# A two-branch layer in fp32: the first block's norm from feature-major tiles alone, and one more step in its scans

## The chip, the cores and the metric

The kernel runs on one core of one Trainium2 chip. The metric is the device time of one execution, in microseconds (us), as the median of three timed executions: 2352.43 us for the kernel before (2352.43, 2354.13 and 2346.6). One more execution was recorded by the hardware profiler, and all views of the trace are of that one.

## The reference

The input is 2048 tokens of 1024 features with 16 learned meta tokens ahead of them. One hybrid layer follows: an RMS norm, one combined projection, a Mamba-2 (SSD) branch and a gated linear attention (GLA) branch beside each other, and a gated merge. What this case touches is the norm at the start and the meta tokens' part of the SSD branch:

```python
def rmsnorm(x, w):
    xf = x.astype(jnp.float32)
    y = xf * lax.rsqrt(jnp.mean(xf * xf, axis=-1, keepdims=True) + EPS)
    return (y * w).astype(x.dtype)

def hybrid_layer(hres, ...):
    u = rmsnorm(hres, norm_w)
    proj = jnp.einsum('bld,dn->bln', u, w_in)
    z, xbc, dt_raw, q, k, v, g_gla, a_lr, merge_g = split_cols(proj, IN_WIDTHS)
...
    s0 = jnp.zeros((b, SSD_HEADS, SSD_HEAD_DIM, SSD_STATE), jnp.float32)
    y_m, s_m = ssd_chunked(xs[:, :m], dt[:, :m], a, bm[:, :m], cm[:, :m], N_META, s0)
    y_r, _ = ssd_chunked(xs[:, m:], dt[:, m:], a, bm[:, m:], cm[:, m:], SSD_CHUNK, s_m)
...
    return hres + jnp.einsum('bld,de->ble', merged, w_out)
```

`m` is 16, so the SSD state after the meta tokens (`s_m`) is the state with which the real tokens begin. Everything is fp32.

## The kernel before

**Stages.** Stage 1 (to about 1550 us of the trace) makes all projections and both branches, in four blocks of 512 tokens; block 0 also has the 16 meta tokens, 528 columns in all. Stage 2 makes the merge gates, the branch projections and the output projection.

**Matmuls.** An fp32 operand is split into a high and a low half of type f32r (ACT copies the high half, another engine subtracts to get the low one), and `accum` (L184 to L188) adds three products: high with high, high with low, low with high. So each projection of a tile is 8 k-tiles times 3 products times the number of its column pieces. In block 0, `load_w` (L164 to L177) also loads each weight raw into a `wr` buffer (SP's DMA queue), splits it on ACT (L173) and POOL (L174) into one of four `whl` buffers, and a later `load_w` stores the pair back to memory (k_...), from which the other blocks load it.

**The start.** `load_u` (L238 to L295) makes u, the normed input, feature-major in 8 column tiles (k-tiles). For block 0 SP first issues the row loads: four of 128 tokens and one of the meta tokens, from `xm`. ACT squares each with an accumulated sum (L250), DVE scales the sum (L259), POOL raises it to −0.5 (L260), and four PE matmuls with the identity (L273), and one for the meta tokens (L277), spread the five factor columns over all partitions in PSUM. Then for each of the 8 column tiles (128 features by 528 tokens, from the transposed copy `xmt`): DMA on SP, two multiplications on DVE (L289, 16 and 512 columns, with the factors in PSUM), the high half on ACT (L291), a store of the normed tile for the next stage on ACT's DMA queue (L292), the low half on DVE (L293). Small constants come behind it: `hv` (L308), three copies of `gw2` into one buffer of the pool "act" (L324), a mask of 448 KB (L331).

**Generators.** In stage 1 the branches' scans are Python generators. The loop over groups and heads runs the projection generators `ssd_proj` and `gla_proj`, and at each of their yields `step()` advances every running scan by one yield. So a yield in a scan decides beside which projection its instructions are put. PE and SP (the queue of weight loads) run in exactly this written order; ACT, DVE and POOL are ordered by the scheduler of the tile framework. The SSD projection of a group is z (token-major, `proj_tok`, with a yield at its half) and four feature tiles (`proj_feat`, one yield each), whose convolution is on DVE (three instructions of L471, then L475).

**The scan.** `ssd_scan` handles the four chunks of 128 tokens of one group. For block 0 it first transposes the meta tokens' rows (L500); one step later come the four score products of the chunks (L516) and `before(0)` (three transposes, L532, and DVE and ACT work on them); then `meta_state` (L506 to L511) multiplies the meta tokens into PSUM (L509) and DVE copies the state to `s_ssd` (L511), directly ahead of `before(1)` and `after(0)`. `after(c)` has the matmuls L556 (within the chunk), L557 (with `s_ssd`) and L559 (the chunk's addition to the state). Behind the last `after` are the row factors (POOL, L230), ACT's scaling (L585) and, a step later, PE's transposes of the finished rows (L590).

**Buffers.** PSUM has three banks for projections (pj), three for transposes (pt) and two for scans (pc). Pools named here: "act" has 8 buffers and "tok4" 5.

## Time and profile before

| what | us |
|---|---|
| runs | 2352.43, 2354.13, 2346.6 (median 2352.43) |
| profiled execution | 2356.86 |
| its span | 2355.0 (1.86 around it) |
| PE busy / DVE busy / ACT busy / POOL busy | 2255.4 / 1562.0 / 1189.1 / 684.2 |
| first matmul of the first projection | 15.74 |
| first matmul of the second projection | 47.49 |

A row of the timeline gives the start and the duration in us, the engine, the line, the operation, the tile written and the tiles read, shapes, and in square brackets the idle time of the engine before it and what ended that. "x8" counts instructions; an fp32 matmul appears as two. A row of the windows gives a stretch and its length, then the busy time of PE, of PE's weight loads, of DVE, ACT and POOL in it, the granted clock of PE as a share of full speed, the busy share of the DMA engines, and GB/s. Groups give busy time, mean ns of one, then idle time before them and its releaser. A row of DMA issues ends with KB and the us from issue to landing.

### The profile page before, as it was taken

To read this page: it belongs to the slowest core of one execution; us is meant where nothing else is said; L and a number is where in the kernel's file an instruction comes from. 1 tells how busy PE (TensorE), PEld (TensorE's weight loads), DVE (VectorE), ACT (ScalarE), POOL (GpSimd) and SP (SyncE) were. 2 spreads that over 40 slices of the span, in tenths; PEclk is the share of its full clock that TensorE was granted. 3 is DMA by queue.
4 is the path that set the end of the run, shared out by engine and by line. 5 is a ranking of instruction groups with operands and counts; after the bars stand their busy time and mean duration, and the time that the engine had idled before them with its cause. 6 is when DMAs were issued, how large, how long until landed. Compare 5 with 4: busy or idle time off the path is not lost.

```text
span 2355.0 us, 36504 instructions
## 1 busy us (share of the span) xinstructions
PE 2255.4 (96%) x12641; PEld 1968.2 (84%) x12641; DVE 1562.0 (66%) x2889; ACT 1189.1 (50%) x2764; POOL 684.2 (29%) x681
## 2 busy tenths in 40 slices
PE   6899999999999999999999999889999999999998
PEld 6889889888888988888988898768788788777886
DVE  4676665676675667566558555664679854788876
ACT  4665655465544455543455443454554454544543
POOL 3343433122321212221122200207424254322441
PEclk8999999999999999999999999989999999999999
DMA  8665875666786666787666655456668866778752
GB/s 274 212 215 183 296 255 192 202 220 218 248 282 191 207 224 208 254 268 221 193 217 216 206 167 163 136 181 226 218 222 275 277 215 213 253 244 274 236 192 108
DMA packets 301546, 518.06 MB, mean 220 GB/s; under 512 B 27696, under 2 KB 143664, under 8 KB 301360
## 3 DMA queue, kind: packets, MB, share of 16 engines
q1 hardware_dynamic: 200112, 402.32, 52.7%
q10 hardware_dynamic: 101248, 113.41, 13.8%
q8 instruction: 99, 1.62, 0.3%
q14 instruction: 87, 0.71, 0.1%
HBM read 368.42 MB, written 147.19 MB: 219 GB/s over the span
## 4 chain that ended last, share of the span: by engine, by line
PE 66%; DMA 12%; DVE 10%; ACT 5%; issue 4%; POOL 2%; SPq 1%; ACTq 0%; DVEq 0%; POOLq 0%
PE pj L186 11%; PE pj L188 11%; PE pj L187 11%; PE psa L186 4%; PE psa L187 4%; PE psa L188 4%; PE psb L187 2%; PE psb L188 2%; PE psb L186 2%; DMA acc<-in_xmt 2%; PE pc L556 2%; DMA br<-br_t 2%; PE pc L690 1%; DVE b L894 1%; PE pc L780 1%
## 5 line engine op out<-in xcount | busy, mean ns | idle before, releaser
L186 PE MATMUL pj<-u,whl 128*128 128x512 f32 (+1 forms) x1184 | 447.4, 378 | 8.3 <-ACT g_all L429 3.3
L188 PE MATMUL pj<-u,whl 128*128 128x512 f32 (+1 forms) x1184 | 431.6, 365 | 0.8 <-POOL whl L174 0.8
L187 PE MATMUL pj<-u,whl 128*128 128x512 f32 (+1 forms) x1184 | 430.7, 364 | 0.0
L186 PE MATMUL pj<-whl,u 128*128 128x256 f32 (+1 forms) x992 | 291.5, 294 | 8.1 <-ACT u L291 5.5
L188 PE MATMUL pj<-whl,u 128*128 128x256 f32 (+1 forms) x992 | 285.2, 287 | 0.7 <-DVE u L293 0.7
L187 PE MATMUL pj<-whl,u 128*128 128x256 f32 (+1 forms) x992 | 285.1, 287 | 0.6 <-POOL whl L174 0.5
L186 PE MATMUL psa<-b,a 128*128 128x512 f32 x640 | 253.5, 396 | 19.0 <-ACT sn L934 17.0
L186 PEld LDWEIGHTS pj<-u,whl 128*128 128x128 f32 x1184 | 225.7, 191 | 46.2 <-ACT g_all L429 3.7
L188 PEld LDWEIGHTS pj<-u,whl 128*128 128x128 f32 x1184 | 225.2, 190 | 36.8 <-POOL whl L174 1.1
L187 PEld LDWEIGHTS pj<-u,whl 128*128 128x128 f32 x1184 | 225.7, 191 | 33.3
L187 PE MATMUL psa<-b,a 128*128 128x512 f32 x640 | 252.8, 395 | 0.0
L188 PE MATMUL psa<-b,a 128*128 128x512 f32 x640 | 252.5, 395 | 0.0
L918 DVE TENSOR_TENSOR a<-ar,a 128x512 fp32r<-128x512 f32 x160 | 151.1, 950 | 82.1 <-ACT a L917 81.9
L186 PEld LDWEIGHTS pj<-whl,u 128*128 128x128 f32 x992 | 192.3, 194 | 9.2 <-ACT u L291 6.0
L187 PEld LDWEIGHTS pj<-whl,u 128*128 128x128 f32 x992 | 192.4, 194 | 1.7 <-POOL whl L174 1.3
L188 PEld LDWEIGHTS pj<-whl,u 128*128 128x128 f32 x992 | 192.4, 194 | 1.5 <-DVE u L293 1.5
L80 POOL TENSOR_TENSOR wr<-wr 128x256 f32<-128x256 f32 x80 | 67.0, 838 | 432.0 <-DMA wr<-y 172.1
L174 POOL TENSOR_TENSOR whl<-wr,whl 128x512 fp32r<-128x512 f32 (+1 forms) x100 | 133.5, 1342 | 188.9 <-ACT whl L173 141.3
L908 POOL TENSOR_TENSOR as<-ar,ar 128x512 f32<-128x512 f32 x40 | 59.3, 1482 | 422.4 <-DMA ar<-in_w_feat 124.3
L894 DVE TENSOR_TENSOR b<-br,b 128x512 fp32r<-128x512 f32 x196 | 149.2, 784 | 45.3 <-ACT b L893 44.8
L471 DVE SCALAR_TENSOR_TENSOR acc<-cin,hcw,acc 128x512 f32<-128x512 f32 (+1 forms) x192 | 156.6, 816 | 24.7 <-ACT acc L467 24.1
L893 ACT ACTIVATE b<-br 128x512 fp32r<-128x512 f32 x196 | 119.1, 626 | 93.5 <-DMA br<-br_t 34.7
(267 smaller groups left out, 5077.9 us busy)
## 6 DMA issues: line engine op xcount, KB each, us to landing
whl<-k_s SPq DMA_DIRECT2D x96, 512.0 KB, 4.4
whl<-k_g SPq DMA_DIRECT2D x96, 512.0 KB, 4.1
whl<-k_v SPq DMA_DIRECT2D x48, 512.0 KB, 3.8
whl<-k_z SPq DMA_DIRECT2D x36, 512.0 KB, 3.8
wr<-in_w_feat SPq DMA_DIRECT2D x64, 256.0 KB, 4.5
k_s<-whl SPq DMA_DIRECT2D x32, 512.0 KB, 3.6
cb<-cumd ACTq DMA_DIRECT2D x64, 256.0 KB, 5.6
y<-gg ACTq DMA_DIRECT2D x64, 256.0 KB, 4.5
```

The source lines that it names most:

```text
L80: nc.gpsimd.tensor_tensor(o, x, y, op=ALU.subtract)
L174: nc.gpsimd.tensor_tensor(hl[:, 1], raw, hl[:, 0].bitcast(F32), op=ALU.subtract)
L186: nc.tensor.matmul(ps, sh, mh, start=first, stop=False, **kw)
L187: nc.tensor.matmul(ps, sh, ml, start=False, stop=False, **kw)
L188: nc.tensor.matmul(ps, sl, mh, start=False, stop=last, **kw)
L471: nc.vector.scalar_tensor_tensor(acc, cin[:, k:k + tt], hcw[:, ti, k:k + 1], acc, op0=ALU.mult, op1=ALU.add)
L556: nc.tensor.matmul(py[:, h * 64:(h + 1) * 64], dm[:, h], xdt[:, h], start=True, stop=True)
L690: nc.tensor.matmul(ps[:, r * P:(r + 1) * P], kq[:, 2 * r * P:(2 * r + 1) * P], kq[:, (2 * r + 1) * P:(2 * r + 2) * P], start=True, stop=True)
L893: nc.scalar.activation(t[:, 0], raw, AF.Copy)
L894: nc.vector.tensor_tensor(t[:, 1], raw, t[:, 0].bitcast(F32), op=ALU.subtract)
L908: nc.gpsimd.tensor_tensor(s1, a21, a22, op=ALU.add)
L918: nc.vector.tensor_tensor(t[:, 1], src, t[:, 0].bitcast(F32), op=ALU.subtract)
```

## The change

1. **First block from columns alone.** `first_u` takes the place of `load_u` for block 0. The row loads from `xm` are gone. The eight column tiles are asked for at once, into eight buffers of the pool "act", the even ones by SP and the odd ones by ACT's queue. ACT squares each tile (L268), seven DVE additions sum them over the k-tiles (L270), five PE matmuls with a column of ones sum over partitions (L275), and one DVE (L277) and one POOL instruction (L279) make all five factor columns. The broadcast to all partitions is the same as before (L282, L284), but ACT copies it into one SBUF tile of 528 columns, so that `to_u` multiplies each tile with one DVE instruction (L248).
2. **Stores of u.** Block 0's stores of the normed tiles go to SP's queue, one behind each raw weight load from the third on, instead of ACT's queue.
3. **A buffer.** The staging of `gw2` comes from the pool "acc" and no longer from "act".
4. **The meta state a step apart.** A `yield` behind `meta_state()` in `ssd_scan`, in block 0 alone: everything of a scan behind the meta state comes one step of `step()` later.

```diff
@@ load_w
             nc.sync.dma_start(raw, src)
+            if u_stores and len(kept) > 2:
+                nc.sync.dma_start(*u_stores.pop(0))
             nc.scalar.activation(hl[:, 0], raw, AF.Copy)
@@ new functions
+    def to_u(b, kt, xk, rbc, uh, ul):
+        m0 = 0 if b else META
+        nc.vector.scalar_tensor_tensor(xk, xk, norm_w[:, kt:kt + 1], rbc, op0=ALU.mult, op1=ALU.mult)
+        nc.scalar.activation(uh[:, kt, :m0 + BLK], xk, AF.Copy)
+        if b:
+            nc.scalar.dma_start(u_left[b][kt], xk[:, m0:])
+        else:
+            u_stores.append((u_left[b][kt], xk[:, m0:]))
+        nc.vector.tensor_tensor(ul[:, kt, :m0 + BLK], xk, uh[:, kt, :m0 + BLK].bitcast(F32), op=ALU.subtract)
+
+    def first_u():
+        tt = META + BLK
+        uh, ul = u_pair(tt)
+        xs = []
+        for kt in range(KT):
+            xs.append(mk(wk, [P, META + BLK], F32, "act", bufs=NACT))
+            (nc.scalar if kt % 2 else nc.sync).dma_start(xs[kt], xmt[:, kt, :tt])
+        nc.sync.dma_start(cst[:, :2], cf32[:, :2])
+        nc.sync.dma_start(pv, pvec)
+        sq = [mk(wk, [P, 2, META + BLK], F32, "tok4", bufs=NT4) for _ in range(KT // 2)]
+        total = sq[0][:, 0]
+        for kt in range(KT):
+            nc.scalar.activation(sq[kt // 2][:, kt % 2], xs[kt], AF.Square)
+            if kt:
+                nc.vector.tensor_tensor(total, total, sq[kt // 2][:, kt % 2], op=ALU.add)
+        at = [META + c * P for c in range(NCH)] + [0]
+        n = len(at)
+        ps = bank(pt, "pt")
+        for i, a in enumerate(at):
+            nc.tensor.matmul(ps[:, 2 * i:2 * i + 2], total[:, a:a + P], ones[:, :2], start=True, stop=True)
+        r = mk(sm, [P, n], F32, "rs5", bufs=1)
+        nc.vector.tensor_scalar(r, ps[:, :2 * n].rearrange("p (i two) -> p i two", two=2)[:, :, 0], 1.0 / D, EPS,
+                                op0=ALU.mult, op1=ALU.add)
+        nc.gpsimd.tensor_tensor(r, r, mhalf[:, 0:1].to_broadcast([P, n]), op=ALU.pow)
+        rb, rm = bank(pt, "pt"), bank(pt, "pt")
+        for c in range(NCH):
+            nc.tensor.matmul(rb[:, c * P:(c + 1) * P], r[:, c:c + 1].to_broadcast([P, P]), ident,
+                             start=True, stop=True)
+        nc.tensor.matmul(rm[:, :META], r[:META, NCH:].to_broadcast([META, P]), ident[:META, :META],
+                         start=True, stop=True)
+        rbc = mk(wk, [P, 3 + META + BLK], F32, "cin")[:, :tt]
+        nc.scalar.activation(rbc[:, :META], rm[:, :META], AF.Copy)
+        nc.scalar.activation(rbc[:, META:], rb, AF.Copy)
+        for kt in range(KT):
+            to_u(0, kt, xs[kt], rbc, uh, ul)
+        return uh, ul
@@ load_u: the part for block 0 taken out
-            if m0:
-                xt = mk(wk, [P, D], F32, "tok4", bufs=NT4)
-                nc.sync.dma_start(xt[:n], xm[r0:r0 + n, :])
-                nc.scalar.activation(xt[:n], xt[:n], AF.Square, accum_out=ss[:n])
...
-    for _ in fetch_u(0):
-        pass
+    next_u[0] = first_u()
@@
-    w2r = mk(wk, [P, META + BLK], F32, "act", bufs=NACT)[:48, :512]
+    w2r = mk(wk, [P, META + BLK], F32, "acc")[:48, :512]
@@ ssd_scan
         if m0:
             meta_state()
+            yield
```

**The order on DVE at the start.** Rows of the order are: line, operation, output and inputs with buffer numbers, shape; x4 counts equal ones. Lines are those of each kernel's own file. Before, from the first multiplication of a column tile on (`acc_298`, `acc_305`, `acc_312` are column tiles, `u_253` holds u, `w_372` the gate weights of gw2):

```order
L289 SCALAR_TENSOR_TENSOR acc_298<-acc_298,pv,pt_291 128x512
L289 SCALAR_TENSOR_TENSOR acc_305<-acc_305,pv,pt_291 128x512
L320 TENSOR_SCALAR nega<-nega 128x16
L289 SCALAR_TENSOR_TENSOR acc_298<-acc_298,pv,pt_296 128x16
L289 SCALAR_TENSOR_TENSOR acc_305<-acc_305,pv,pt_296 128x16
L327 TENSOR_TENSOR w_372<-act_368,w_372 16x512
L332 CAST msk<-tok_29_376 128x896
L293 TENSOR_TENSOR u_253<-acc_298,u_253 128x528
L293 TENSOR_TENSOR u_253<-acc_305,u_253 128x528
L289 SCALAR_TENSOR_TENSOR acc_312<-acc_312,pv,pt_296 128x16
L289 SCALAR_TENSOR_TENSOR acc_312<-acc_312,pv,pt_291 128x512
```

In the change, from the last addition of squares on (`tok_11_272` the sum, `act_254` to `act_268` the eight column tiles, `cin_307` the factor tile):

```order
L270 TENSOR_TENSOR tok_11_272<-tok_11_272,tok_14_275 128x528
L360 CAST msk<-tok_21_356 128x896
L277 TENSOR_SCALAR rs_16_297<-pt_291 128x5
L248 SCALAR_TENSOR_TENSOR act_254<-act_254,pv,cin_307 128x528
L248 SCALAR_TENSOR_TENSOR act_256<-act_256,pv,cin_307 128x528
L248 SCALAR_TENSOR_TENSOR act_258<-act_258,pv,cin_307 128x528
L248 SCALAR_TENSOR_TENSOR act_260<-act_260,pv,cin_307 128x528
L248 SCALAR_TENSOR_TENSOR act_262<-act_262,pv,cin_307 128x528
L248 SCALAR_TENSOR_TENSOR act_264<-act_264,pv,cin_307 128x528
L248 SCALAR_TENSOR_TENSOR act_266<-act_266,pv,cin_307 128x528
L248 SCALAR_TENSOR_TENSOR act_268<-act_268,pv,cin_307 128x528
L254 TENSOR_TENSOR u_253<-act_254,u_253 128x528
```

Each tile's low half (L293) came behind the tile's multiplications before; now all eight multiplications stand ahead of the first low half (L254), and the last addition behind the gate weights (L355, the row ahead of these).

**The order on PE at the meta state of group 0.** Before, behind the last matmul of a feature tile's projection (`pj_1133`, `pj_1134` its banks):

```order
L188 MATMUL pj_1134<-u_253,whl_1166 128x264
L509 MATMUL pc_1211<-c_120_1081,bt_1083 128x256
L532 MATMUL pt_1216<-cst,act_673 128x128
L532 MATMUL pt_1216<-cst,act_763 128x128
L532 MATMUL pt_1216<-cst,act_849 128x128
L556 MATMUL pc_1234<-c_128_1100,sq_1107 128x64 x4
L557 MATMUL pc_1234<-s_ssd,act_927 128x256
L559 MATMUL pc_1240<-c_129_1102,bt_1105 128x256
L186 MATMUL pj_1257<-u_253,whl_1259 128x264
```

In the change, the same place (L537 is the line that was L509; `pj_1208` and `pj_1209` are the banks of the next projection):

```order
L190 MATMUL pj_1122<-u_253,whl_1154 128x264
L537 MATMUL pc_1199<-c_112_1069,bt_1071 128x256
L188 MATMUL pj_1208<-u_253,whl_1210 128x264
L189 MATMUL pj_1208<-u_253,whl_1210 128x264
L190 MATMUL pj_1208<-u_253,whl_1210 128x264
L188 MATMUL pj_1209<-u_253,whl_1210 128x264
L189 MATMUL pj_1209<-u_253,whl_1210 128x264
L190 MATMUL pj_1209<-u_253,whl_1210 128x264
L188 MATMUL pj_1208<-u_253,whl_1210 128x264
```

The transposes, chunk products and state matmuls that followed the meta state directly now stand behind the 48 matmuls of the next projection.

**The order on PE at the end of group 0's scan.** Before, behind the last matmul of group 1's z (`pj_1613`); `tok_124_1092` holds the finished rows:

```order
L188 MATMUL pj_1613<-whl_1698,u_253 128x256
L590 MATMUL pt_1757<-cst,tok_124_1092 128x128 x4
L590 MATMUL pt_1765<-cst,tok_124_1092 128x128 x4
L500 MATMUL pt_1773<-cst,act_1208 16x128
L500 MATMUL pt_1773<-cst,act_1332 16x128
L500 MATMUL pt_1773<-cst,act_1453 16x128
L516 MATMUL pc_1781<-act_1585,act_1453 128x128 x4
L532 MATMUL pt_1792<-cst,act_1208 128x128
L532 MATMUL pt_1792<-cst,act_1332 128x128
L532 MATMUL pt_1792<-cst,act_1453 128x128
L186 MATMUL pj_1810<-u_253,whl_1812 128x264
```

In the change, the same place, and then the end of the next projection:

```order
L190 MATMUL pj_1584<-whl_1679,u_253 128x256
L528 MATMUL pt_1745<-cst,act_1196 16x128
L528 MATMUL pt_1745<-cst,act_1283 16x128
L528 MATMUL pt_1745<-cst,act_1404 16x128
L544 MATMUL pc_1753<-act_1538,act_1404 128x128 x4
L560 MATMUL pt_1764<-cst,act_1196 128x128
L560 MATMUL pt_1764<-cst,act_1283 128x128
L560 MATMUL pt_1764<-cst,act_1404 128x128
L188 MATMUL pj_1782<-u_253,whl_1784 128x264
```

```order
L190 MATMUL pj_1783<-u_253,whl_1815 128x264
L619 MATMUL pt_1860<-cst,tok_116_1080 128x128 x4
L619 MATMUL pt_1868<-cst,tok_116_1080 128x128 x4
L537 MATMUL pc_1876<-c_218_1749,bt_1751 128x256
L188 MATMUL pj_1879<-u_253,whl_1881 128x264
```

The eight transposes of finished rows (L590, now L619) have moved from ahead of group 1's scan steps to behind the next projection (banks `pj_1782` and `pj_1783`), where they stand ahead of group 1's meta state.

More of the change, by code (lines that the diff above doesn't have):

```diff
@@ L235, in split, with u_pair @@
         nc.vector.tensor_tensor(lo, src, h.bitcast(F32), op=ALU.subtract)
-    def load_u(b):
-        m0 = META if b == 0 else 0
-        row0 = META - m0 + b * BLK
-        tt = m0 + BLK
-        pair = mk(upool, [P, 2, KT * (META + BLK)], F32R, "u")[:, :, :KT * tt]
-        uh, ul = [pair[:, i].rearrange("p (k t) -> p k t", k=KT) for i in range(2)]
+    u_stores = []
+    def u_pair(tt):
+        pair = mk(upool, [P, 2, KT * (META + BLK)], F32R, "u")[:, :, :KT * tt]
+        return [pair[:, i].rearrange("p (k t) -> p k t", k=KT) for i in range(2)]
@@ L264, in load_u @@
         for c in range(NCH):
[L265 removed]
+            rs.append(rows_rstd(row0 + c * P, P))
             yield
[L267 to L270 removed]
         rb = bank(pt, "pt")
@@ L273, in load_u @@
             nc.tensor.matmul(rb[:, c * P:(c + 1) * P], rs[c].to_broadcast([P, P]), ident, start=True, stop=True)
[L274 to L293 removed]
+        rbc = mk(wk, [P, 3 + META + BLK], F32, "cin")[:, :BLK]
+        nc.scalar.activation(rbc, rb, AF.Copy)
+        yield
+        for kt in range(KT):
+            xk = mk(wk, [P, META + BLK], F32, "acc")[:, :BLK]
+            nc.sync.dma_start(xk, xmt[:, kt, row0:row0 + BLK])
+            to_u(b, kt, xk, rbc, uh, ul)
             yield
@@ L576, in ssd_scan @@
             meta_state()
+            yield
         for c in range(1, NCH):
```

39 lines of the change are left out of this document (8 added, 31 removed).

## The prediction

> **What bounds the kernel now.** I read the page first, then the timeline of the first 150 us, then the two-microsecond windows around its gaps, then the groups by form for prices.
>
> ```profile
> PE 2255.4 (96%) x12641; PEld 1968.2 (84%) x12641; DVE 1562.0 (66%) x2889; ACT 1189.1 (50%) x2764; POOL 684.2 (29%) x681
> ```
>
> PE is busy 96% of the span, and the change leaves its matmul work almost as it is. So only what keeps PE idle, or slow, can change: 2355.0 − 2255.4 = 100 us of idle time in the whole span. The edit touches three places of it: the start, and two stops in the first scan of block 0. The start first, from the timeline of the first 50 us (start, duration, engine, line; in brackets the idle time before and what ended it):
>
> ```profile
> 9.51 1.25 SPq L324 DMA_DIRECT2D act<-in_gw  x3
> 10.06 2.26 PE L273 MATMUL pt<-cst,rs 128*128 128x128 f32 x8 [10.06 <-DMA cst<-in_cf]
> 12.55 0.61 PE L277 MATMUL pt<-cst,rs 16*128 16x16 f32 x2 [0.22 <-POOL rs L260]
> 13.15 0.63 ACT L326 ACTIVATE w<-act 48x512 fp32r<-48x512 f32 x1 [0.42 <-DMA act<-in_gw]
> 14.16 0.68 DVE L327 TENSOR_TENSOR w<-act,w 16x512 fp32r<-16x512 f32 x1
> 15.74 0.61 PE L186 MATMUL pj<-whl,u 128*128 128x288 f32 x1 [2.58 <-ACT whl L173]
> 15.76 2.98 POOL L174 TENSOR_TENSOR whl<-wr,whl 128x288 fp32r<-128x288 f32 x3 [3.27 <-DMA wr<-in_w_zm]
> 24.03 0.29 PE L186 MATMUL pj<-whl,u 128*128 128x288 f32 x1
> 24.16 0.29 PE L187 MATMUL pj<-whl,u 128*128 128x288 f32 x1
> 30.10 0.61 PE L186 MATMUL pj<-whl,u 128*128 128x288 f32 x1 [2.58 <-ACT u L291]
> 40.01 0.61 PE L186 MATMUL pj<-whl,u 128*128 128x288 f32 x1 [2.04 <-ACT u L291]
> 42.43 0.44 PE L188 MATMUL pj<-whl,u 128*128 128x288 f32 x1
> 42.67 0.44 PE L186 MATMUL pj<-whl,u 128*128 128x288 f32 x1
> 47.49 0.37 PE L186 MATMUL pj<-u,whl 128*128 128x264 f32 x1
> ```
>
> The reader is to see that the first projection runs from 15.74 to 47.49, though its 120 matmuls need 120 × 0.13 = 15.6 us at the quick pace (24.03 to 24.16). It waits for u, column tile after column tile (2.58 and 2.04), and each wait drops it to the slow pace (42.43 to 42.67: 0.24).
>
> **The change, the head.** Prices, from the DMA issues of the first 30 us, a window, and the groups by form of the first 160 us:
>
> ```profile
> 9.51 1.06 ACT L250 ACTIVATE tok<-tok 128x1024 f32<-128x1024 f32 x1 [0.86 <-DMA tok<-in_xm]
> act<-in_gw SPq DMA_DIRECT2D x3, 32.0 KB, 3.0
> 5.00:10.00 5.00, 0.00 (x0) 0.00 (x0) 0.46 (x3) 3.64 (x7) 1.66 (x3) 1.00 1.04 356
> L291 ACT ACTIVATE u<-acc 128x528 fp32r<-128x528 f32 x8 | 5.0, 642 | 5.7 <-DVE acc L289 5.2 <-DMA wr<-in_w_zm 0.4
> L293 DVE TENSOR_TENSOR u<-acc,u 128x528 fp32r<-128x528 f32 x8 | 6.9, 878 | 1.5 <-ACT u L291 1.4
> 114.02 0.76 DVE L471 SCALAR_TENSOR_TENSOR acc<-cin,hcw,acc 128x528 f32<-128x528 f32 x1
> 114.70 0.42 DVE L564 TENSOR_TENSOR c<-pc,ecu 128x256 f32<-128x256 f32 x1
> ```
>
> It removes the four row loads of 512 KB (and one of 64 KB) that came ahead of the eight column tiles, so 2.1 MB less come before the first factor. But the eight tiles are 2.1 MB too, and at the window's 356 GB/s (last column; the one before it, 1.04, is the DMA engines' share) they take 6 us: begun at about 2 to 3 us, the last lands near 9, where now ACT gets the last large row tile at 9.5 (L250). The gain is that u's tiles are then all there at once, and that the waits of the first projection go. What is late next is a row of small work, in the new order of DVE, POOL and ACT. I follow it:
> - The last add of squares stands behind the copy of gw2 on DVE. gw2's third load was issued up to 10.7; with the queue emptied sooner I take 8.2, and its 3.0 us give 11.2. ACT's copy 0.63 gives 11.85, DVE's subtraction 0.68 gives 12.5, the add (by L293's form) 0.8 gives 13.3.
> - Five PE matmuls by the price of L273 (2.26 us for four, 0.565 each): 2.8, to 16.1, when the queue has long held nothing else. DVE's scale 0.15. POOL's pow stands behind three splits of weights (2.98, L174), which begin when the weights land, now at 15.76; with the queue emptied sooner I take 13.8, so that the pow starts at 16.8 and takes 1.0 by the four-column row L230 below: 17.9.
> - The broadcast costs 2.26 + 0.61 as now, to 20.8, and ACT's copy of it to SBUF some 0.2 more behind PE's last part: 21.0.
> - The new order has all eight multiplications ahead of the first subtraction. Their form is that of L471: the next DVE instruction starts 0.68 behind it, so 8 × 0.70 = 5.6, to 26.6 (from below 0.6, from above L293's 0.878, 7.0). ACT's copies (0.642 each) fit beside them. The first subtraction gives u's low half at 27.35, without which PE's third product can't run.
> - Then 15.6 us of matmuls, with a cold beginning. The windows of the next part show cold stretches of 3.4 and 6.8 us; at 0.24 in place of 0.13 each microsecond loses 0.46, so 1.6 to 3.1, of which I take the middle, 2.3. PE is through at 45.3 in place of 47.49: **−2.2**. If gw2 and POOL are early it is −5; if the tiles land as late as the row tiles and the multiplications go at 0.878, it is +1.
>
> The squares (8 × 0.64 on ACT, seven adds on DVE) run while tiles still land and cost nothing unless the tiles come sooner than 0.8 us apart. The moved u stores leave ACT's queue, and each waits on SP ahead of a weight load until DVE has made its tile; all eight are made by 26.6, and the fourth of the eight weight loads is wanted by PE only three eighths through the projection, at some 34, so I cost them at nothing. By the window's rate, 264 KB more ahead of a load are 0.75 us, and that is the price if this cover goes.
>
> One sentence of the Trainium skill speaks against the first edit: "Trainium Kernel Development and Optimization", Key Constraints, says that DMAs of the SP, ACT and POOL queues share 16 DMA engines, so that several queues save only the issue time of a sequencer. The window above agrees, with a share of 1.04 from one queue; by this rule asking from two queues brings no tile sooner, which is how I have reckoned, and a result by which the head gains nothing is a rival.
>
> **The scan, first stop.** The timeline around the first scan step after the meta state, and the windows of two microseconds (busy time of PE, PEld, DVE, ACT, POOL, then granted clock, DMA share and GB/s):
>
> ```profile
> 98.67 0.55 PE L532 MATMUL pt<-cst,act 128*128 128x128 f32 x3
> 99.06 1.00 PE L556 MATMUL pc<-c,sq 128*128 128x64 f32 x8
> 100.37 2.79 DVE L437 TENSOR_TENSOR_SCAN g_all<-ones_r,tok 128x16 f32<-128x16 f32 x10
> 101.03 0.56 ACT L467 ACTIVATE acc<-pj,hcb,hcw 128x264 f32<-128x264 f32 x1
> 103.09 0.39 DVE L511 COPY s_ssd<-pc 128x256 f32<-128x256 f32 x1
> 103.53 1.22 PE L557 MATMUL pc<-s_ssd,act 128*128 128x256 f32 x2 [3.47 <-DVE s_ssd L511]
> 112.49 0.49 PE L532 MATMUL pt<-cst,act 128*128 128x128 f32 x3
> 100.00:102.00 2.00, 0.06 (x1) 0.00 (x0) 2.00 (x8) 1.09 (x5) 0.00 (x0) 0.85 0.69 248
> 102.00:104.00 2.00, 0.47 (x1) 0.47 (x2) 2.00 (x7) 1.98 (x6) 1.03 (x2) 0.50 0.48 150
> 108.00:110.00 2.00, 2.00 (x18) 2.00 (x17) 0.40 (x1) 0.16 (x1) 0.00 (x0) 0.94 0.06 20
> ```
>
> L557 reads the state that L511 copies out of PSUM, and L511 stands on DVE behind ten scans of the gates (L437). PE waits 3.47 us, and the clock falls to 0.50: 0.85 in the first window means 0.6 us cold, so from 101.4; 0.94 in the last means 0.24, so to 108.24. With the yield, the meta state's matmuls come here, and then the next projection at once; L532 to L557 come that projection later, when the state is long copied. PE would thus stop for nothing of the scan, but for a bank: its second half of columns takes the bank that ACT still reads at 101.03 to 101.59. From 99.05 (98.67, where the meta state's matmuls are through, and 0.36 for three matmuls of the first half) that leaves 2.55 idle. Then 45 matmuls at 0.12 (0.13 by 264/288 of the columns), 5.4, to 107.0, and the scan step, 0.39 + 1.0 + 0.75 = 2.15, to 109.15, against 112.49 now: −3.3 if the clock stays up. Before, it fell 1.35 us into the stop (100.06 to 101.4), so I take it to fall again, and the cold work that follows to last between 3.4 us and the 4.7 of before (103.53 to 108.24); half of 4.0 is lost: **−1.3**. The bounds are −3.3 and 0.
>
> The Trainium skill has a rule here, "TensorE: Matmul & The Clock Gate", Part 1: The HAM clock gate: windows of 3413 ns that run freely, and a fall only after at least one idle window. The drop here and the one at the second stop came sooner after PE's last work than that, so the trace doesn't bear out the length, though 101.4, 108.24 and the next part's two edges lie whole windows apart within 0.05; by the rule 2.55 us would not reach, and that is a rival.
>
> **The scan, second stop.** The same two views at the end of the scan of group 0:
>
> ```profile
> 142.61 0.28 PE L188 MATMUL pj<-whl,u 128*128 128x256 f32 x1
> 144.15 1.02 POOL L230 TENSOR_TENSOR rstd<-rstd,mhalf 128x4 f32<-128x4 f32 x1
> 145.77 2.53 PE L590 MATMUL pt<-cst,tok 128*128 128x128 f32 x8 [2.87 <-ACT tok L585]
> 148.09 0.85 PE L500 MATMUL pt<-cst,act 128*16 128x128 f32 x3
> 150.09 0.37 PE L186 MATMUL pj<-u,whl 128*128 128x264 f32 x1
> 144.00:146.00 2.00, 0.23 (x1) 0.18 (x1) 0.66 (x2) 0.80 (x2) 1.06 (x2) 0.94 0.94 294
> 146.00:148.00 2.00, 2.00 (x8) 1.40 (x8) 0.06 (x1) 2.00 (x6) 0.44 (x1) 0.50 0.89 333
> 148.00:150.00 2.00, 2.00 (x15) 1.77 (x14) 1.04 (x2) 2.00 (x5) 2.00 (x2) 0.71 0.16 66
> ```
>
> PE's transposes of the finished rows (L590) wait for ACT's scaling, and that for POOL's pow, which is 2.87 us, and a cold stretch from 145.76 (0.94) to 149.16 (0.71). Between 142.9 (142.61 + 0.28) and 150.09 PE begins no projection: 7.2 us. In the new order these transposes stand behind the 48 matmuls of the next projection, some 6 us later, when their rows are ready. Of the 7.2 stay 1.8 for the next scan's own matmuls (148.3 to 150.09), 0.8 that I allow for a bank which DVE frees, and 1.35 for the transposes at the quick pace (half of 2.53, and a little): **−3.2**, with 0 and −4.5 as ends. Its cover is the one projection of shift; if DVE is later than that, the stop is there again.
>
> The later scans of block 0 move in the same way, beside a PE that is full there, and I count nothing for them; from block 1 on the order is the old one.
>
> **Sum.** −2.2 − 1.3 − 3.2 = −6.7 us. On the profiled execution, 2356.86 (its span of 2355.0 and 1.86 around it), that is 2350.2. That execution lies 4.4 above the median of the runs, 2352.43, so the time to expect is 2352.43 − 6.7 = **2345.7**.
>
> **The rivals.**
> 1. *The clock stays up at the first stop* (the page's rule above, or a stop that falls well between two edges). For it speaks that the idle time is 0.9 shorter than before; against it the drop after 1.35 us. −2.2 − 3.3 − 3.2 = −8.7: 2343.7. Chance 0.20.
> 2. *The head gains nothing*, because the chain through gw2, POOL's pow and eight multiplications ends where the waits of now end. For it speak the window's full DMA share and five engine changes in a row; against it the 16 us that the first projection now loses. Only the scans remain, −4.5: 2347.9. Chance 0.20.
> 3. *DVE falls behind in the later scans and the second stop comes back in all of them.* The yield puts block 0's scan work later by a step, onto the next group's. If DVE, which decides when POOL's pow may start, is more than about a projection (48 matmuls at 0.12, 5.8 us) behind, the transposes of L619 wait in each group: the first keeps its stop, and three more get one of 2.87 and 1.7 for the cold stretch, 3 × 4.6 = 13.8, less the 3.5 of the head and the first stop: +10.3, 2362.7. For it speaks DVE with 2.00 of 2.00 in the windows at 100 and 102; against it 0.40 and 0.66 in those at 108 and 144, so that it catches up. Chance 0.08.
> 4. *The head gains more*: gw2 lands by 10 and the pow gets ahead of the splits, −5, and the scans −4.5: −9.5, 2342.9. Chance 0.12.
>
> **How the numbers follow.** My forecast has 0.35, and 0.05 is left for cases near no change. About 0.3%, 7.06 us, is what a measurement of this kernel can tell from no change, and −6.7 lies next to it. So of my forecast's 0.35 I put 0.15 to faster; with rivals 1 and 4 that is 0.47. The other 0.20, rival 2 and the rest are 0.45 within it, and rival 3 is 0.08 slower. The range goes down to rivals 1 and 4 together (−11.5) with 3.4 for the scatter of the runs, 2337.5, and up to rival 2 with 5 for the scatter, 2353; rival 3 is left out.
>
> **What would show it.** In the profile of after, the first 264-column matmul starts near 45.3 (47.49 now); later than 48 means that the head's chain was longer than I made it, and its timeline names the step. The wait of L557's successor for s_ssd is gone, a wait of some 2.5 for ACT's evacuation stands near 99, and the clock there says which of forecast and rival 1 holds. The transposes of L619 wait for nothing, at their new place in group 0 and in the three others; waits of 2 us there are rival 3. What would make it wrong altogether: a new stop after 152, where I have counted none.

## The result, and the profile after

The changed kernel takes 2346.81 us (median of 20 runs, 2340.09 to 2354.96) where the kernel before takes 2356.1 (median of 20). The ratio is 0.9967, 95% interval [0.9954, 0.9980]: faster by 0.33%, or 7.8 us of 2356.1 (4.7 to 10.8 by the interval; the two medians alone lie 9.3 apart). The forecast was −6.7 us. It started from three runs with a median of 2352.43, 3.7 below that of the 20, so the difference is the figure to compare, and not the 2345.7. The profiled execution of the changed kernel has a span of 2348.2, 6.8 less than that of before. The sum was right; the parts that made it were not all right, and most of this document is on that.

The page of the changed kernel, busy time by engine:

```profile
PE 2253.1 (96%) x12651; PEld 1966.1 (84%) x12651; DVE 1566.5 (67%) x2884; ACT 1188.2 (51%) x2764; POOL 684.1 (29%) x677
```

PE's busy time is 2.3 us less (cold stretches are part of it), and idle time on it 95.1 in place of 99.6 (span less busy). The timeline of the changed kernel's start:

```profile
12.09 0.71 DVE L270 TENSOR_TENSOR tok<-tok,tok 128x528 f32<-128x528 f32 x1
12.95 2.26 PE L275 MATMUL pt<-ones_r,tok 128*128 128x2 f32 x10 [12.95 <-DVE tok L270]
16.03 1.18 POOL L279 TENSOR_TENSOR rs<-rs,mhalf 128x5 f32<-128x5 f32 x1
19.28 0.61 PE L284 MATMUL pt<-cst,rs 16*128 16x16 f32 x2
20.14 5.52 DVE L248 SCALAR_TENSOR_TENSOR act<-act,pv,cin 128x528 f32<-128x528 f32 x8 [4.72 <-ACT cin L287]
25.57 5.03 DVE L254 TENSOR_TENSOR u<-act,u 128x528 fp32r<-128x528 f32 x8
26.33 0.61 PE L190 MATMUL pj<-whl,u 128*128 128x288 f32 x1 [3.85 <-DVE u L254]
30.58 0.44 PE L189 MATMUL pt<-whl,u 128*128 128x288 f32 x1
30.82 0.44 PE L190 MATMUL pt<-whl,u 128*128 128x288 f32 x1
31.24 0.29 PE L189 MATMUL pt<-whl,u 128*128 128x288 f32 x1
31.37 0.29 PE L190 MATMUL pt<-whl,u 128*128 128x288 f32 x1
44.56 0.39 PE L188 MATMUL pj<-u,whl 128*128 128x264 f32 x1 [0.81 <-ACT alr L395]
```

The chain of the prediction can be ticked off: last addition at 12.09 (forecast 12.5), PE's sums from 12.95 (13.3), the pow at 16.03 (16.8), the spreading over at 19.9 (20.8), eight multiplications in 5.52 (5.6), the third product's first matmul at 26.33 (27.35). PE then runs cold (30.58 to 30.82: 0.24) until about 31, quick from 31.24 (0.13), and without a wait for u. The second projection starts at 44.56 in place of 47.49.

For what follows I measure PE between the same matmuls of the projections in each kernel (the numbers 120, 408, 530, 800, 1150, 1300, 1470 and 1690 of stage 1, counted by their records; all kernels have 6744). The windows of the kernel before, cut there (stretch, length, busy time of PE, PEld, DVE, ACT and POOL, granted clock, DMA share, GB/s):

```profile
47.50:87.10 39.60, 39.30 (x323) 38.39 (x322) 23.28 (x35) 25.18 (x61) 18.85 (x18) 1.00 0.75 260
87.10:117.70 30.60, 24.01 (x155) 22.71 (x155) 21.58 (x46) 19.75 (x52) 8.37 (x9) 0.83 0.52 164
117.70:168.40 50.70, 47.20 (x357) 44.39 (x356) 36.55 (x69) 35.30 (x90) 20.21 (x20) 0.97 0.65 218
168.40:224.40 56.00, 55.69 (x448) 54.40 (x447) 41.24 (x73) 33.76 (x90) 25.88 (x27) 1.00 0.60 198
224.40:255.80 31.40, 28.07 (x186) 26.28 (x185) 11.21 (x29) 18.83 (x52) 9.41 (x11) 0.89 0.69 244
255.80:294.10 38.30, 38.28 (x239) 34.03 (x238) 33.62 (x66) 21.21 (x54) 18.72 (x17) 1.00 0.82 287
294.10:342.60 48.50, 43.41 (x284) 38.70 (x283) 34.93 (x64) 27.38 (x66) 18.39 (x14) 1.00 0.75 261
```

And those of the changed kernel, between the same matmuls:

```profile
44.60:86.00 41.40, 39.61 (x322) 38.52 (x322) 23.62 (x38) 25.78 (x64) 19.38 (x19) 1.00 0.84 290
86.00:113.90 27.90, 22.24 (x141) 21.25 (x141) 19.54 (x38) 19.17 (x48) 7.30 (x8) 0.82 0.56 180
113.90:166.30 52.40, 47.98 (x356) 45.73 (x356) 37.26 (x71) 35.79 (x91) 20.66 (x21) 0.93 0.63 211
166.30:222.60 56.30, 55.77 (x449) 54.50 (x448) 40.26 (x74) 33.21 (x88) 27.66 (x26) 1.00 0.59 197
222.60:250.30 27.70, 26.57 (x193) 24.82 (x192) 14.03 (x34) 19.22 (x54) 9.90 (x12) 1.00 0.73 251
250.30:289.30 39.00, 39.00 (x247) 34.83 (x246) 30.22 (x60) 22.44 (x57) 19.15 (x16) 1.00 0.88 312
289.30:336.70 47.40, 44.01 (x283) 39.48 (x282) 39.41 (x69) 27.14 (x68) 20.24 (x14) 0.98 0.75 258
```

Two things are to be seen. The second stretch is 2.7 shorter, but PE has 14 records fewer in it: a scan step was put off, and comes back as 7 and 8 records more in the fifth and sixth. So lengths alone mislead, and I count what PE **loses** in a stretch: its idle time (length less busy), and half of its busy time while the granted clock is 0.50 (a matmul then takes 0.24 for 0.13). And the third stretch, where −3.2 was forecast, is longer by 1.7, while the fifth, where nothing was forecast, is shorter by 3.7.

### The profile page after: what moved, and what is told of

Its sections match the earlier page's. It is cut to its first block, busy times and chain, and to the rows that moved or that the text cites. A ratio compares the mean times of both kernels' runs of the same rounds, so it can differ in the third digit from the quotient of the medians.

```text
span 2348.2 us, 36518 instructions
## 1 busy us (share of the span) xinstructions
PE 2253.1 (96%) x12651; PEld 1966.1 (84%) x12651; DVE 1566.5 (67%) x2884; ACT 1188.2 (51%) x2764; POOL 684.1 (29%) x677
## 4 chain that ended last, share of the span: by engine, by line
PE 39%; DMA 5%; DVE 4%; issue 2%; ACT 2%; SPq 0%; POOL 0%; ACTq 0%; DVEq 0%; POOLq 0%
PE psa L188 5%; PE psa L190 4%; PE psa L189 4%; PE pj L188 4%; PE pj L190 4%; PE pj L189 4%; PE psb L188 2%; PE psb L189 2%; PE psb L190 2%; DMA br<-br_t 2%; PE psc L188 1%; PE psc L189 1%; PE psc L190 1%; DMA br<-gate_t 1%; DVE b L923 1%
## 5 line engine op out<-in xcount | busy, mean ns | idle before, releaser
L923 DVE TENSOR_TENSOR b<-br,b 128x512 fp32r<-128x512 f32 x196 | 149.1, 783 | 48.4 <-ACT b L922 47.5
```

Of the source, the lines that this page charges most:

```text
L923: nc.vector.tensor_tensor(t[:, 1], raw, t[:, 0].bitcast(F32), op=ALU.subtract)
```

## The experiments

Each of these kernels was profiled once and timed beside the kernel before. The table has all of them: the start of the second projection, then PE's loss in the stretches above (first, second, and so on; worked out from the trace as just said), their sum, and the ratio to the kernel before with its interval.

| kernel | 2nd proj. | 1 | 2 | 3 | 4 | 5 | 6 | 7 | sum | ratio |
|---|---|---|---|---|---|---|---|---|---|---|
| before | 47.5 | 0.3 | 10.6 | 5.2 | 0.3 | 6.3 | 0 | 5.1 | 27.8 | 1 |
| the change | 44.6 | 1.8 | 10.0 | 7.2 | 0.5 | 1.1 | 0 | 4.3 | 24.9 | 0.9967 [0.9954, 0.9980] |
| e11 the change again | 43.9 | 2.1 | 7.7 | 6.8 | 0.5 | 0.8 | 0 | 2.6 | 20.5 | 0.9947 [0.9928, 0.9965] |
| e1 yield only | 49.0 | 1.9 | 10.4 | 7.1 | 0.5 | 0.6 | 0 | 3.8 | 24.3 | 0.9972 [0.9956, 0.9989] |
| e2 head only | 43.6 | 1.7 | 10.0 | 6.5 | 0.3 | 5.0 | 0.1 | 6.7 | 30.3 | 0.9988 [0.9973, 1.0003] |
| e3 DVE by hand | 40.9 | 2.1 | 7.2 | 6.7 | 0.4 | 1.1 | 0 | 3.4 | 20.9 | 0.9933 [0.9911, 0.9956] |
| e4 one queue | 43.4 | 1.4 | 10.2 | 7.4 | 0.5 | 0.9 | 0 | 3.3 | 23.7 | 0.9943 [0.9923, 0.9964] |
| e5 yield in group 3 | 44.6 | 2.0 | 10.0 | 5.1 | 0.3 | 6.7 | 0 | 3.0 | 27.1 | 0.9971 [0.9956, 0.9986] |
| e6 yield in 0, 1, 2 | 44.1 | 1.7 | 10.1 | 7.3 | 0.5 | 1.6 | 3.2 | 6.2 | 30.6 | 0.9978 [0.9965, 0.9990] |
| e7 yield in group 0 | 43.2 | 1.7 | 7.3 | 3.1 | 0.3 | 5.2 | 0.1 | 7.0 | 24.7 | 0.9965 [0.9953, 0.9978] |
| e8 e3 and e4 | 40.1 | 1.2 | 8.6 | 6.4 | 0.5 | 1.5 | 0 | 2.9 | 21.1 | 0.9946 [0.9926, 0.9966] |
| e9 yield in 0, 2, 3 | 43.9 | 1.7 | 7.3 | 3.1 | 0.1 | 1.5 | 0 | 3.7 | 17.4 | 0.9939 [0.9916, 0.9962] |
| e10 stores on ACT | 42.9 | 0.2 | 7.2 | 6.9 | 0.5 | 1.2 | 0 | 4.0 | 20.0 | 0.9944 [0.9921, 0.9966] |
| e12 e8 and e9 | 40.2 | 1.3 | 7.2 | 3.1 | 0.2 | 2.0 | 0 | 3.4 | 17.2 | 0.9913 [0.9884, 0.9941] |

The ratios' intervals are about ±0.2%, some 4 us, so that neighbours in the table are rarely told apart by time; the stretches tell them apart.

The start of the second projection scatters as well: the seven profiles with the change's head, its two queues and its stores (the change, e11, e2, e5, e6, e7, e9) have 43.2 to 44.6, and the two with the head of before 47.5 and 49.0. In e1 the cold stretch of the start lasts to 52.4 (46.8 before), and that is its 1.9 in stretch 1.

**e1, the yield alone, in the kernel before**

```diff
         if m0:
             meta_state()
+            yield
```

> The kernel before with the yield behind meta_state alone. Theory (the yield and the head add up): the head stays (first 264-column matmul at 47.5 us), PE waits about 2.5 us for ACT's evacuation near 101.6 where it waited 3.47, and by the last feature tile of group 1 (landmark: DVE's last convolution step, 141.6 in before) the lead is 1.5 to 3 us; then a new stop of about 4 us near 157, as in the changed kernel near 155, takes the gain of the second stop back; time 2 to 5 us below the kernel before. Rival (the yield carries the whole gain): 6 to 8 us below. Rival (the yield only moves stops): within 1 us.

The ratio says −0.28%, 6.6 us, which is above the theory's 2 to 5 and in the rival's 6 to 8, though its interval takes in most of both. The new stop came, 4.25 us at 159.82. The gain is in stretch 5, which neither text had.

**e2, the head alone**

```diff
             meta_state()
-            yield
```

> The changed kernel without the yield. Theory: first 264-column matmul near 44.6 us (2.9 earlier than before), the stop of L557's kind for s_ssd (3.5) and the one of the transposes of finished rows (2.9) are back, no stop near 155, and behind 160 the lead over before is what the head gave, 1.5 to 3 us; time 2 to 4 us below before. Rival (the head carries the whole gain): 6 to 8 us below.

As the theory said: the second projection starts at 43.6, both stops of the scan are back (2.51 and 2.89), nothing of 4 us is near 155, and the time is 2.8 us less (0.12%), with an interval that takes in zero. By the two ratios the yield carries the larger part of the change, but their intervals overlap; 6.6 and 2.8 add up to 9.4 where 7.8 was measured, within the intervals.

**e3, DVE's order at the start by hand**: the low half of a tile behind the multiplication of the next one.

```diff
-        for kt in range(KT):
-            to_u(0, kt, xs[kt], rbc, uh, ul)
+        def low(kt):
+            nc.vector.tensor_tensor(ul[:, kt], xs[kt], uh[:, kt].bitcast(F32), op=ALU.subtract)
+
+        with tc.manual_schedule(engines={mybir.EngineType.DVE}):
+            for kt in range(KT):
+                nc.vector.scalar_tensor_tensor(xs[kt], xs[kt], norm_w[:, kt:kt + 1], rbc, op0=ALU.mult, op1=ALU.mult)
+                nc.scalar.activation(uh[:, kt], xs[kt], AF.Copy)
+                u_stores.append((u_left[0][kt], xs[kt][:, META:]))
+                if kt:
+                    low(kt - 1)
+            low(KT - 1)
```

> The changed kernel with DVE's order in the first block written by hand: the low half of a tile directly behind the multiplication of the next tile. Theory (the eight multiplications ahead of the first low half are what the first projection waits for): PE's third product starts near 22.4 us in place of 26.33 and the first 264-column matmul near 41 in place of 44.56, 3 to 4 us earlier. Rival (weights or the cold clock limit the projection anyway): it starts at 44 or later, and PE waits for weights or u inside the projection.

As the theory said. The wait of 3.85 us for the first low half is gone, and the timeline of this kernel has the second projection 3.6 us earlier than in the changed kernel:

```profile
40.92 0.39 PE L188 MATMUL pj<-u,whl 128*128 128x264 f32 x1 [0.90 <-ACT alr L404]
```

So the eight multiplications ahead of the first subtraction, which the scheduler chose, cost the change about as much as its head gained: 3.6 us against 2.9 by the first profile, 2.9 against 3.6 by e11's. The time of this kernel also has the clock on its side: in stretch 2 it loses 7.2 in place of 10.0, by a clock fall that did not come (see the first stop below).

**e4, one queue**

```diff
-            (nc.scalar if kt % 2 else nc.sync).dma_start(xs[kt], xmt[:, kt, :tt])
+            nc.sync.dma_start(xs[kt], xmt[:, kt, :tt])
```

> The changed kernel with all eight column tiles asked for by SP's queue. Theory (the DMA engines limit, not the issue): first 264-column matmul within 0.5 us of 44.56. Rival (issue limits: 0.5 us each, so the last tile is asked for some 2 us later): the last square and what hangs on it 1 to 2 us later, 45.5 to 46.5.

The first profile has one queue 1.2 us earlier at the second projection, which neither text had; but 43.4 lies inside the scatter of this head (43.2 to 44.6), so that gain is not shown by this run alone. With DVE by hand it is 0.7 to 0.9 (40.9 in e3; 40.1 and 40.2 with one queue, in e8 and e12). What is clear lies earlier. The DMA issues up to 22 us and the last two squares, first of the changed kernel:

```profile
act<-in_xmt ACTq DMA_DIRECT2D x4, 264.0 KB, 5.5
act<-in_xmt SPq DMA_DIRECT2D x4, 264.0 KB, 5.3
```

```profile
8.91 1.18 ACT L268 ACTIVATE tok<-act 128x528 f32<-128x528 f32 x2 [0.18 <-DMA act<-in_xmt]
```

and of the kernel with one queue, here with the last addition, the sums of squares on PE and the gate weights:

```profile
act<-in_xmt SPq DMA_DIRECT2D x8, 264.0 KB, 4.2
```

```profile
8.46 1.36 ACT L268 ACTIVATE tok<-act 128x528 f32<-128x528 f32 x2 [0.25 <-DMA act<-in_xmt]
10.28 0.70 DVE L270 TENSOR_TENSOR tok<-tok,tok 128x528 f32<-128x528 f32 x1
11.04 2.29 PE L275 MATMUL pt<-ones_r,tok 128*128 128x2 f32 x10 [11.04 <-DVE tok L270]
11.76 0.68 DVE L355 TENSOR_TENSOR w<-acc,w 16x512 fp32r<-16x512 f32 x1 [0.62 <-ACT w L354]
```

A tile takes 4.2 us from issue to landing with one queue and 5.3 to 5.5 with two, but with two the later tiles are also asked for earlier. The first square starts at 3.54 in place of 4.68, and the last one ends at 9.82 in place of 10.09 (10.11 in e8 and 10.05 in e12, which have one queue too). So the second queue makes the first tiles later and the last one no earlier. The sums on PE start 1.9 earlier, and most of that is order and not DMA: in this kernel the scheduler put the last addition (10.28) ahead of the gate weights (11.76), in the change behind them (12.09). The pow then waits for two weight splits on POOL, so that 1.2 is left at its start (14.83 in place of 16.03). The sentence of the Trainium skill ("Trainium Kernel Development and Optimization", Key Constraints) that queues share the DMA engines agrees with the end of the last square.

**e5 and e6, which group's yield removes the wait near 235.** The kernel before waits 2.49 and 0.84 us for weights at 237 to 239; the changed one waits 0.40 there.

```diff
             meta_state()
-            yield
+            if g == SG - 1:
+                yield
```

That is e5; in e6 the condition is `g < SG - 1`.

> The changed kernel with the yield in group 3's scan alone. Stretches are measured between the same projection matmuls of PE (numbers 408, 530, 800, 1150, 1300, 1470 and 1690 of the projections). Theory (the scan step that the yield puts off stands where PE waited for weights behind group 3): first and second stop as in the kernel before (stretches near 30.3 and 51.3 us), no stop near 235 (stretch 27.7 in place of 30.8 to 31.4) and the stops of 298 to 311 smaller; lead over before at number 1690 about 6 us, time 5 to 9 us below before. Rival (the stop near 237 is SP's row load waiting for a buffer, and its going is due to the earlier groups): stretch 30 or more, time 2 to 4 us below before.

> The changed kernel with the yield in the scans of groups 0 to 2 and not in 3. Theory (put-off step of group 3): the first two stretches as in the changed kernel (27.9 and 52.5), the wait for weights near 235 back (2.5 and 0.8; stretch 30 or more), time 1 to 4 us below before. Rival (earlier groups): no wait for weights there, stretch 27.7.

My theory fell: with group 3 alone (first row, e5) the wait stays, and with groups 0 to 2 (the other two, e6) it is down to 0.43, with 0.84 behind it, while the stop of 300, which e5 doesn't have, is back. The times, 6.8 and 5.2 us below before, do not decide: e5's even lies in the theory's range.

```profile
236.34 0.59 PE L188 MATMUL pj<-u,whl 128*128 128x264 f32 x1 [3.16 <-ACT whl L175]
```

```profile
235.07 0.39 PE L188 MATMUL pj<-u,whl 128*128 128x264 f32 x1 [0.43 <-ACT whl L175]
299.36 0.66 PE L738 MATMUL pt<-cst,act 128*128 128x128 f32 x4 [2.10 <-ACT gg L622]
```

I had put the wrong scan there. Read in the changed kernel's timeline, what stands ahead of the weights' wait is a step of group 2's scan:

```profile
233.38 1.00 PE L584 MATMUL pc<-c,sq 128*128 128x64 f32 x8
234.22 0.65 PE L585 MATMUL pc<-s_ssd,act 128*128 128x256 f32 x2
234.70 0.59 PE L587 MATMUL pc<-c,bt 128*128 128x256 f32 x2
```

Over all kernels, stretch 5 loses 0.6 to 2.0 us wherever group 2 has its yield (the change, e1, e3, e4, e6, e8 to e12) and 5.0 to 6.7 wherever it hasn't (before, e2, e5, e7). No run has group 2's yield alone, so that it does this without the others isn't shown. The weights come late there because SP waits for a buffer for the next block's rows (16.2 us in the kernel before); a step of scan work that was put off now fills PE's wait. Group 3's yield does the like near 300: stretch 7 loses 2.6 to 4.3 with it, and 5.1 to 7.0 without it. e6 also shows a new stop of 1.47 us at 254 and a cold stretch, 3.2 in stretch 6, where group 2 is late and group 3 is not.

**e7, the yield in group 0 alone**

```diff
-            yield
+            if g == 0:
+                yield
```

> The changed kernel with the yield in group 0's scan alone. Theory (the new stop near 155 is group 1's put-off scan work on ACT ahead of the evacuation): no stop of 4 us near 155; the second stretch (about 52.5 in the changed kernel, 51.3 without the yield) near 48.5, since the transposes of finished rows wait no more and nothing takes their place. Rival (group 0's late end alone brings the stop): it stays, stretch 52 or more.

The stop of 4 us is gone and no clock fall is left in stretch 3 (loss 3.1 in place of 7.2), so group 0's late end alone does not make it; e9 will show that it is group 1's yield. The length is 50.6, not 48.5: two smaller waits took its place, 0.5 and 1.73 us. The changed kernel's timeline shows the stop:

```profile
148.79 1.04 PE L619 MATMUL pt<-cst,tok 128*128 128x128 f32 x8
153.11 1.28 ACT L572 ACTIVATE sq<-cb,tkc 128x128 f32<-128x128 f32 x4 [0.67 <-DMA cb<-cumd]
154.56 0.55 ACT L495 ACTIVATE acc<-pj,hcb,hcw 128x264 f32<-128x264 f32 x1
155.17 0.59 PE L188 MATMUL pj<-u,whl 128*128 128x264 f32 x1 [4.16 <-ACT acc L495]
```

The transposes of the finished rows (148.79) wait for nothing, as forecast. But ACT works on group 1's decay factors (L572) before it empties the bank (L495) that the next projection needs. PE stops for 4.16 us, and the clock is at 0.50 from 154.0 to 160.9. The same two rows of ACT in this kernel, which has no such stop:

```profile
149.20 1.28 ACT L572 ACTIVATE sq<-cb,tkc 128x128 f32<-128x128 f32 x4 [0.72 <-DMA cb<-cumd]
150.65 0.56 ACT L495 ACTIVATE acc<-pj,hcb,hcw 128x264 f32<-128x264 f32 x1
```

So the theory had the right group and the wrong path. ACT's order is the same with and without group 1's yield, and it begins to empty the bank as late: 5.61 us behind the end of the last projection in the change (148.95 to 154.56), 5.67 here (144.98 to 150.65), 5.5 to 5.8 in all eleven kernels with group 0's yield, and 0.6 or less in the three without. It is PE that is early: from the scaling of group 0's rows to this emptying ACT needs 9.5 us in the change and 9.8 in the kernel before (145.02 to 154.56, 146.91 to 156.69), but PE is no longer held by the transposes. Without group 1's yield PE fills the time with group 1's chunk products and the two small waits (146.98 to 151.51 here); with it that work is put off, and PE stands before the bank.

**e8, e3 and e4 together**

> The hand-written DVE order and the single queue together. Theory (both gains lie in one chain, one ahead of the factor and the other behind it): first 264-column matmul near 39.7 us (40.9 with the order alone, 43.4 with the queue alone), time 15 to 18 us below before. Rival (weights come too late for the earlier start): near 41, time as with the order alone.

The second projection starts at 40.1, 0.9 earlier than with the order alone and 0.4 behind the theory's 39.7, and the time is not told apart from e3's. The theory's 15 to 18 was not reached (0.54%, 12.7 us; interval 8 to 17).

**e9, the yield in groups 0, 2 and 3**

```diff
-            yield
+            if g != 1:
+                yield
```

> The changed kernel with the yield in the scans of groups 0, 2 and 3, and not in group 1. Stretches between projection matmuls 408, 530, 800, 1150, 1300, 1470, 1690. Theory (group 1's put-off step makes the stop near 155, group 2's fills the wait near 235, group 3's the waits near 300): no stop of 4 us near 155, second stretch 50.6 (52.5 in the changed kernel), the fourth 27.7 to 28.5, the last 47 or less; time 1 to 3 us below the changed kernel. Rival (the later groups' gain hangs on the whole chain of put-off steps): the wait of 2.5 for weights near 235 comes back, stretch 30 or more, time as the changed kernel or above.

As the theory said, in the stretches: the loss is 3.1 in the third and 1.5 in the fifth, 17.4 in all, against 24.9 and 20.5 of the changed kernel's two profiles. By time it is not told apart from e11 beside it. Only group 1's yield is left out here, so the stop of 4 us hangs on it. The small wait that takes the stop's place is that for the state, which the yield removed in group 0:

```profile
151.01 0.70 PE L585 MATMUL pc<-s_ssd,act 128*128 128x256 f32 x2 [1.73 <-DVE s_ssd L539]
```

**e10, the stores of u on ACT's queue again**

```diff
-        if b:
-            nc.scalar.dma_start(u_left[b][kt], xk[:, m0:])
-        else:
-            u_stores.append((u_left[b][kt], xk[:, m0:]))
+        nc.scalar.dma_start(u_left[b][kt], xk[:, m0:])
```

> The changed kernel with block 0's stores of u on ACT's queue again, behind each high half. Theory (part 2 costs nothing and gives nothing, since the low halves wait for the eight multiplications): first 264-column matmul within 0.5 us of 44.56, time within 2 us of the changed kernel. Rival (the issues, 0.4 us each, hold up ACT's copies, and 2 MB of stores run against the weight loads): 45.5 or later.

Neither: the second projection starts at 42.9, the earliest of the kernels with this head and two queues (43.2 to 44.6), and stretch 1 loses 0.2 in place of 1.8 and 2.1. The time, 2.5 us below e11's beside it, is not told apart from it. In the changed kernel it has this stop (timeline):

```profile
63.13 1.97 ACTq L512 DMA_DIRECT2D cb<-cumd  x3
66.05 0.39 PE L188 MATMUL pj<-u,whl 128*128 128x264 f32 x1 [1.79 <-ACT acc L495]
```

ACT is held by three DMA issues (1.97 us) ahead of emptying a bank. With the stores away from SP these issues start at 60.07 and the stop is gone. That the move costs 1.6 to 1.9 there is shown, and the other kernels agree: the waits for ACT in stretch 1 add up to 1.0 to 2.1 us in the eleven with the moved stores and to 0.2 to 0.3 in the three without (before, e1, e10). The path is argued from the timelines: weights that SP asks for later, ACT's work in another order behind them.

**e11, the changed kernel once more**

> The changed kernel once more, for the scatter of its stretches: the stops up to 345 us at the same instructions as in the first profile, each stretch up to there within 1 us of it (22.9, 41.4, 27.9, 52.5, 56.2, 27.7, 39.0, 47.4), except where the clock falls otherwise; stage 2 may differ by 5 us. Rival (the stops are chance): different instructions.

The stops of more than 1 us are at the same instructions, and six of the eight times agree within 1 us. Stretch 7 is 45.4 in place of 47.4, and stretch 2 is 25.7 in place of 27.9. First the first profile's stop (timeline, then windows), then the second's:

```profile
100.45 0.59 PE L188 MATMUL pj<-u,whl 128*128 128x264 f32 x1 [2.55 <-ACT acc L495]
98.00:100.00 2.00, 0.00 (x0) 0.00 (x0) 2.00 (x5) 0.54 (x3) 0.70 (x1) 0.86 0.24 96
100.00:102.00 2.00, 1.55 (x7) 1.55 (x8) 2.00 (x8) 1.85 (x6) 0.53 (x2) 0.50 0.96 285
```

```profile
100.33 0.39 PE L188 MATMUL pj<-u,whl 128*128 128x264 f32 x1 [1.65 <-ACT acc L495]
98.00:100.00 2.00, 0.68 (x4) 0.42 (x3) 2.00 (x5) 0.67 (x3) 0.57 (x1) 1.00 0.31 123
100.00:102.00 2.00, 1.67 (x13) 1.68 (x14) 2.00 (x8) 1.84 (x7) 0.65 (x2) 1.00 0.90 270
```

**e12, the best of the parts**: DVE by hand, one queue, the yield in all groups but 1.

> Hand-written DVE order, one queue, and the yield in all groups but 1. Theory (the gains add up): first 264-column matmul near 40, no stop near 150, time 1 to 3 us below the kernel with order and queue alone, 14 to 18 below before. Rival (no more than the head's gains): ratio as that kernel, 0.993 to 0.995.

0.9913 [0.9884, 0.9941], 20 us below the kernel before (its median in these runs 2357.35, this one's 2337.41): the lowest ratio of all, and the smallest loss, 17.2. The theory had 14 to 18 us. Its interval lies below that of the change's 20 runs, but overlaps with e11's and with those of its parts (e3, e4, e8, e9), so that the gains add up is not shown by time. The stores on ACT's queue, which e10 found better, were not tried together with it.

## Why the prediction was right, point by point

- **The head, −2.2: right, −2.9.** Each step of the chain came within 1.1 us of its forecast. Over the seven profiles with this head it is −2.9 to −4.3, against the 47.5 of the one profile of before. Its place as a bound was shown by e3: with the low halves interleaved the same chain ends 3.6 earlier.
- **The moved stores, "at nothing": wrong.** My cover was that all tiles are made by 26.6 and the fourth load is wanted at 34. I looked only at the first projection. The price came behind it: ACT empties a bank late there, and stretch 1 loses 1.5 more than before (e10: 0.2 without the move).
- **The first stop, −1.3 with −3.3 as a bound: the mechanism was right to the digit** (idle 2.55, the bank, L495), **the clock fell or stayed up by chance.** Stretch 2 loses 0.6 less in the first profile, where the clock fell at 99.4, and 2.9 less in the second, where it stayed up. That was rival 1, and it has its turn: of eleven profiles with group 0's yield the clock fell at this stop in five and stayed up in six. The draw is made one stop earlier. At the stop of 3.1 us at 85 to 94, which all of them have, the cold stretch lasted 3.4 us in the five and 6.8 in the six. After the longer one PE came later to the bank and stood there for 1.2 to 1.7 us; after the shorter one for 2.3 to 3.3.
- **The second stop, −3.2: wrong.** The old place did better than forecast: 1.3 us between the projections (141.4 to 142.7), where the sum left 1.8 and 0.8. The step that failed is the price of the new place, "1.35 for the transposes at the quick pace" and nothing else. The rows were ready, as forecast, but the next projection needs a bank that ACT frees 5.6 us behind the last one, and group 1's yield had put off the work of PE that covered this time: PE stood 4.16 us, the clock fell, and stretch 3 loses 2.0 more than before. It is also the sign that I had named for a forecast wrong altogether, "a new stop after 152". It is not rival 3, in which DVE is late and the transposes wait in each group. e7 and e9 take the stop away by leaving out group 1's yield, and stretch 3 then loses 2.1 less than before.
- **The later scans, "beside a PE that is full there, and I count nothing for them": wrong.** PE was not full: stretches 5 and 7 lost 6.3 and 5.1 us, in waits that the prediction doesn't name. The put-off steps fill them: −5.2 and −0.8 in the first profile.
- **The sum.** −2.9 + 1.5 − 0.6 + 2.0 + 0.2 − 5.2 − 0.8 = −5.8 up to matmul 1690, which is at 336.7 in place of 342.6. The rest of the span is 0.9 shorter. In e11 that rest is 2347.2 − 331.0 = 2016.2, against 2011.5 in the first profile of the same kernel, so 0.9 there is scatter. That the total was right is luck: a gain I had not counted stood against losses I had not seen.

## What to carry to other kernels

A yield that puts work off does not only remove the wait in front of it: ask of every later stop on the bound engine whether the work that is put off now lies in it, and what it covered in the place that it leaves: the bound engine comes sooner to the next bank there, and the engine that empties it may be no sooner. Compare two traces between the same instructions by idle and cold time, since lengths change with work that is only moved. And look at the order that the scheduler makes inside a new chain: the order on one engine (e3) was worth about as much as the change's head.

## What the runs showed of the hardware

The granted clock at a stop of PE depends on where the stop lies, and not on its length alone. At one later instruction, the product with the GLA branch's state (`s_gla`, at 324 to 327 us), PE stopped for 2.29 us in four kernels; the clock fell in e3 (327.6) and e10 (327.0) and stayed at 1.00 in e9 and e12. The cold stretches of these traces last 3.41 us or whole multiples of it, so I count on in such steps from each trace's last change of the clock: a step ends inside the stop in e9 (326.5) and e12 (323.3), and behind it in e3 and e10. At the first stop of the scan the clock fell 1.5 us into a stop of 2.55 (97.9 to 99.4, the changed kernel). The Trainium skill ("TensorE: Matmul & The Clock Gate", Part 1: The HAM clock gate) has the clock fall after at least one idle window of 3413 ns; the length of the cold stretches here, 3.4 and 6.8, agrees with its window, but the fall in a stop shorter than one window doesn't, and the measurement decides.

Asking for the same eight tiles from two queues made the first come 1.1 us later (squares from 4.68 in place of 3.54) and the last no earlier (its square ends at 10.09; at 9.82, 10.11 and 10.05 with one queue).
